# A decoder layer on one core: a wider vector tile and another order of the tile pools

## Chip, cores and metric

The kernel runs on one core of a Trainium2 chip. The metric is device time in microseconds (us) for one execution, from the first instruction to the last and what lies around them. The engines are TensorE (PE in the profile; PEld is its loading of the stationary operand), VectorE (DVE), ScalarE (ACT), GpSimd (POOL) and SyncE (SP, which issues nearly all DMAs). Operands of products lie in the on-chip memory, 128 partitions wide; an address is a byte offset within each partition.

## What is computed

One layer of a decoder trunk, fp32 in and out, for 512 tokens of 1024 features:

```
h = x + 1/2 * SwiGLU_1(RMSNorm(x))                     D_FF 2816
n = RMSNorm(h);  P = n @ W_in + b_in                   1024 -> 6 x 1024
    A: GLU -> causal depthwise conv (31) -> LayerNorm -> swish -> w_a
    B: GELU -> u, v -> LayerNorm(v) -> chunked causal gating u * (W_s v + b) -> w_b
h = h + (sigmoid(gate_A) * y_A + sigmoid(gate_B) * y_B) @ W_out
h = h + CrossAttn(RMSNorm(h), RMSNorm_mem(mem))        4 heads, 256 memory tokens
h = h + 1/2 * SwiGLU_2(RMSNorm(h))
y = RMSNorm_final(h)
```

## The kernel before

Features lie on the partitions and the 512 tokens along them, so a residual or operand tile is 128 x 512. Each matrix product is made of three: activation and weight are each split into a high part (type fp32r) and the rest (fp32r too), and `mm3` adds high by high, high by low and low by high into one PSUM tile (lines 103 to 106). `linear` takes a column tile of weights as the stationary operand and moves the activations (512 columns, 256 for the memory); `linear_rows` (lines 172 to 174) does the reverse, so that there the weights move and the activations are loaded. `linear` works through blocks of 8 K tiles: one DMA of 512 KB into `raw` (4 buffers), then `wsplit`: ScalarE writes `whi` (line 96), VectorE the rest `wlo` (line 97), three buffers each, then 24 products.

The stages in order are: FFN 1 (44 column tiles up, `g` and `u`; 8 down, `d`), the keys of the memory (`pk`), the gated channels (`av`, `ag`), the token-major halves of the input projection (`r`), the spatial gating (`pm`, transposes `pt`) between the products of `gate_b`, `yb`, `ga`, the memory's values, `ya`, `o`, the attention (`pq`, scores `sc`, transposes `ptt`, weighted values `po`, `wo`), FFN 2, and the final norm by halves (`dl`). The convolution (line 344, 30 steps of VectorE for each of 8 channel tiles) stands in pieces behind the blocks of weights from the gated channels on; how many go behind a block is decided by `spend` from the constants MM_US (the three products of a K tile), SPLIT_US (VectorE's part of a block's split) and OP_US (another VectorE operation). The order on each engine is fixed when the program is built.

Where a tile lies follows from the pools, which are laid out one after the other in the order in which they are opened. `const` begins at byte 16512, which is 128 past a multiple of 256. Its first tile is `vec`, all vectors as columns (356 columns of 4 bytes), then `h`, the split activations `xhi` and `xlo`, `ident`, `ones`, `avg` and `mhalf`, four columns of -0.5 that `pow_mhalf` (line 196, on POOL) takes as exponent. `wpool` holds the weights, `tmp` the short-lived tiles, among them some of 4 to 32 bytes, and `big` 50 slots of 128 x 512 for everything else that products read: the split hidden activations `f`, the memory `m`, keys, values, queries, probabilities. Bytes past a multiple of 256, as the programs are built:

| operands | before | after |
|---|---|---|
| `h`, `xhi`, `xlo`, `ident`, `ones`, `avg` | 32 | 0 |
| weights `raw`, `whi`, `wlo` | 64 | 0 |
| slots of `big` | 96 | 0 |
| `acc` and the other tiles `ev` of `tmp` | 64 | 0 |
| `rb` tiles of `tmp` | 224 | 160 |

## Time and profile before

| | |
|---|---|
| median of 3 runs | 1356.39 us (1355.55 to 1356.74) |
| the profiled execution | span 1355.1 us |
| PE busy | 1332.3 us, 98%, 5968 products |
| PEld busy | 1079.1 us, 80% |
| DVE busy | 777.9 us, 57% |
| ACT busy | 456.5 us, 34% |
| DMA | 132.47 MB, mean 98 GB/s |

The profile is of one execution; its span is the time from the first to the last instruction, 1.3 us under the median of the runs. Busy time is the union of an engine's instructions. A matmul's end is modelled and lies beyond the start of the next, so how fast products follow each other is read from their starts, or from how many fall in a stretch, and not from their mean duration. VectorE's instructions overlap in the same way at their ends. An fp32 product of 512 columns is recorded as two instructions.

### The profile page before, as it was taken

What the parts mean: (1) busy time and instruction counts of PE and PEld (TensorE: products, weight loads), DVE (VectorE), ACT (ScalarE), POOL (GpSimd) and SP (SyncE); (2) the same over time, 40 slices, a digit from 0 to 9 for tenths busy, and PEclk for the clock granted to TensorE, in tenths of its full rate; (3) what the DMA queues carried; (4) which work ended last, traced back from release to release, by engine and by line L of the source; (5) the groups of instructions that cost most, each with busy time, mean ns of one, the idle gap of its engine ahead of it and who ended that gap; (6) DMA issues with size and microseconds to landing.
All of it is one profiled execution on the core that took longest, in us unless ns stands there. A gap on an engine that the chain in (4) does not pass through costs nothing.

```text
span 1355.1 us, 14923 instructions
## 1 busy us (share of the span) xinstructions
PE 1332.3 (98%) x5968; PEld 1079.1 (80%) x5968; DVE 777.9 (57%) x1078; ACT 456.5 (34%) x618; POOL 19.4 (1%) x31
## 2 busy tenths in 40 slices
PE   7999999999999999999999999999999999999996
PEld 6788888888898888888787788887878888888886
DVE  5544444434367999998996775554644444442323
ACT  5322222223233223343224743334432222222221
POOL 0000000000020000100000000000000000000000
PEclk9999999999999999999999999999999999999998
DMA  6333333233353332322233333202332333323321
GB/s 207 109 94 93 94 93 94 86 96 109 114 181 115 94 94 94 101 97 76 92 94 116 102 109 109 62 20 76 123 93 93 94 94 93 94 86 101 86 70 62
DMA packets 40660, 132.47 MB, mean 98 GB/s; under 512 B 4432, under 2 KB 7248, under 8 KB 40592
## 3 DMA queue, kind: packets, MB, share of 16 engines
q1 hardware_dynamic: 39872, 129.17, 30.9%
q0 software_dynamic: 720, 2.36, 0.6%
q8 instruction: 46, 0.75, 0.2%
q14 instruction: 22, 0.18, 0.0%
HBM read 129.42 MB, written 2.10 MB: 97 GB/s over the span
## 4 chain that ended last, share of the span: by engine, by line
PE 97%; DVE 1%; ACT 1%; DMA 0%; issue 0%; SPq 0%; DVEq 0%; POOLq 0%; ACTq 0%
PE u L106 6%; PE g L104 6%; PE u L105 6%; PE g L105 6%; PE g L106 6%; PE u L104 6%; PE d L106 6%; PE d L104 6%; PE d L105 6%; PE r L173 2%; PE r L172 2%; PE r L174 2%; PE ya L104 1%; PE ya L105 1%; PE o L105 1%; PE av L105 1%
## 5 line engine op out<-in xcount | busy, mean ns | idle before, releaser
L344 DVE SCALAR_TENSOR_TENSOR cv<-ap,vec,cv 128x494 f32<-128x494 f32 (+24 forms) x240 | 163.3, 729 | 0.4
L244 DVE TENSOR_TENSOR u<-u,n4rb 128x512 f32<-128x512 f32 x22 | 15.2, 692 | 70.3 <-PE u L106 70.3
L244 DVE TENSOR_TENSOR u<-u,n1rb 128x512 f32<-128x512 f32 x20 | 13.8, 691 | 65.8 <-PE u L106 65.8
L240 DVE TENSOR_TENSOR g<-g,n4rb 128x512 f32<-128x512 f32 x22 | 15.2, 692 | 51.7 <-PE g L106 47.5
L240 DVE TENSOR_TENSOR g<-g,n1rb 128x512 f32<-128x512 f32 x20 | 13.8, 691 | 43.3 <-PE g L106 43.3
L246 DVE TENSOR_TENSOR f<-s,u 128x512 f32<-128x512 f32 x44 | 30.4, 692 | 5.4 <-ACT s L242 1.1
L261 DVE SCALAR_TENSOR_TENSOR h<-d,h 128x512 f32<-128x512 f32 x15 | 10.4, 692 | 31.5 <-PE d L106 31.5
L242 ACT ACTIVATE s<-g 128x512 f32<-128x512 f32 x44 | 27.8, 633 | 0.1
L192 DVE TENSOR_TENSOR acc<-acc,sq 128x512 f32<-128x512 f32 x34 | 23.3, 685 | 0.1
L191 ACT ACTIVATE sq<-h 128x512 f32<-128x512 f32 x34 | 21.2, 624 | 1.4 <-DVE h L261 0.2
L184 DVE SCALAR_TENSOR_TENSOR xlo<-h,vec,xhi 128x512 fp32r<-128x512 f32 x24 | 17.7, 746 | 5.3 <-ACT xhi L183 5.2
L183 ACT ACTIVATE xhi<-h,vec 128x512 fp32r<-128x512 f32 x24 | 17.2, 717 | 1.9 <-DVE h L626 1.0
L543 DVE TENSOR_TENSOR h<-o,h 128x512 f32<-128x512 f32 x8 | 5.5, 692 | 13.7 <-PE o L106 13.7
L532 DVE TENSOR_TENSOR ga<-ya,sga 128x512 f32<-128x512 f32 x8 | 5.5, 690 | 13.4 <-PE ya L106 13.4
L387 DVE TENSOR_TENSOR uv<-r,br 128x512 f32<-128x512 f32 x16 | 10.7, 686 | 0.1
L104 PE MATMUL fg<-xhi,first0h 128*128 128x512 f32 x4 | 2.2, 553 | 7.8 <-ACT first0h L96 7.8
L587 ACT ACTIVATE pr<-sc,mx 128x256 f32<-128x256 f32 x16 | 7.4, 470 | 6.4 <-DVE mx L584 6.3
L567 DVE TENSOR_TENSOR qt<-pq,n3rb 128x512 f32<-128x512 f32 x8 | 5.3, 687 | 7.3 <-ACT n3rb L218 4.3
L626 DVE TENSOR_TENSOR h<-wo,h 128x512 f32<-128x512 f32 x8 | 5.4, 688 | 7.0 <-PE wo L106 7.0
L388 ACT ACTIVATE uv<-uv 128x512 f32<-128x512 f32 x16 | 9.0, 621 | 0.6 <-DVE uv L387 0.6
L583 DVE TENSOR_REDUCE mx<-sc 128x2 f32<-128x512 f32 x8 | 5.5, 692 | 3.7 <-PE sc L106 3.3
L97 DVE TENSOR_TENSOR d1w8l<-d1w,d1w8h 128x1024 fp32r<-128x1024 f32 x2 | 2.5, 1226 | 8.7 <-ACT d1w8h L96 8.7
(4300 smaller groups left out, 4279.4 us busy)
## 6 DMA issues: line engine op xcount, KB each, us to landing
h<-xT SPq DMA_DIRECT2D x8, 256.0 KB, 5.9
first<-w_gu SPq DMA_DIRECT2D x8, 256.0 KB, 6.1
d0w<-w_dn SPq DMA_DIRECT2D x4, 512.0 KB, 3.5
d1w<-w_dn SPq DMA_DIRECT2D x4, 512.0 KB, 3.7
d2w<-w_dn SPq DMA_DIRECT2D x4, 512.0 KB, 3.4
d3w<-w_dn SPq DMA_DIRECT2D x4, 512.0 KB, 3.5
d4w<-w_dn SPq DMA_DIRECT2D x4, 512.0 KB, 3.6
d5w<-w_dn SPq DMA_DIRECT2D x4, 512.0 KB, 3.4
```

The lines of the kernel that those rows point to most:

```text
L104: PE.matmul(out, whi, ahi, start=start, stop=False)
L105: PE.matmul(out, whi, alo, start=False, stop=False)
L106: PE.matmul(out, wlo, ahi, start=False, stop=stop)
L172: PE.matmul(accs[t], a_h, whi[:, k - k0, :], start=k == 0, stop=False)
L173: PE.matmul(accs[t], a_h, wlo[:, k - k0, :], start=False, stop=False)
L174: PE.matmul(accs[t], a_l, whi[:, k - k0, :], start=False, stop=k == nk - 1)
L192: V.tensor_tensor(out=acc, in0=acc, in1=sq, op=ALU.add)
L240: V.tensor_tensor(out=g1, in0=pg, in1=rb, op=ALU.mult)
L242: S.activation(s1, g1, AF.Silu)
L244: V.tensor_tensor(out=u1, in0=pu, in1=rb, op=ALU.mult)
L246: V.tensor_tensor(out=f, in0=s1, in1=u1, op=ALU.mult)
L344: V.scalar_tensor_tensor(out=o, in0=aps[i][:, :T - back], scalar=w, in1=o, op0=ALU.mult, op1=ALU.add)
```

## The change

The tile `vec` gets 416 columns (1664 bytes) in place of 356; the load fills the first 356 as before. `mhalf` is no tile of its own any more but four of the new columns of `vec`. The pool `big` is opened before `tmp`, so that the tiles of a few bytes lie behind everything that products read. `const` now puts `h` at byte 18176, and from there on all tiles up to those small ones have lengths that are multiples of 256. No instruction is added, removed or moved on any engine: the built programs have the same rows in the same order with the same waits, but for the name `vec` in place of `mhalf` on POOL. Comments and docstrings are dropped as well, which changes line numbers alone.

```diff
@@ -42,6 +42,7 @@
     VOFF[_n] = _o
     _o += _w
 NV = _o
+VW = 416
...
@@ -52,12 +53,13 @@
     const = ctx.enter_context(tc.tile_pool(name="const", bufs=1))
     wpool = ctx.enter_context(tc.tile_pool(name="wpool", bufs=1))
+    big = ctx.enter_context(tc.tile_pool(name="big", bufs=1))
     tmp = ctx.enter_context(tc.tile_pool(name="tmp", bufs=1))
-    big = ctx.enter_context(tc.tile_pool(name="big", bufs=1))
...
-    vec = const.tile([P, NV], F32, name="vec")
+
+    vec = const.tile([P, VW], F32, name="vec")
...
-    mhalf = const.tile([P, TT], F32, name="mhalf")
+    mhalf = vec[:, NV:NV + TT]
...
-            nc.sync.dma_start(out=vec, in_=vecs)
+            nc.sync.dma_start(out=vec[:, :NV], in_=vecs)
```

## Rows read from the trace of the kernel before

**Rows 1.** The page: span, busy time by engine, granted clock in 40 slices, chain.

```profile
span 1355.1 us, 14923 instructions
...
PE 1332.3 (98%) x5968; PEld 1079.1 (80%) x5968; DVE 777.9 (57%) x1078; ACT 456.5 (34%) x618; POOL 19.4 (1%) x31
...
PEclk9999999999999999999999999999999999999998
...
PE 97%; DVE 1%; ACT 1%; DMA 0%; issue 0%; SPq 0%; DVEq 0%; POOLq 0%; ACTq 0%
```

**Rows 2.** The waits of PE: us in total, times, longest us.

```profile
PE fg L104 <- ACT first0h L96: 7.8, 1, 7.8
PE nf1c L206 <- ACT sq L673: 2.5, 1, 2.5
PE po L104 <- ACT ph L179: 2.3, 4, 0.6
PE nf1b L214 <- DVE nf1d L212: 1.7, 1, 1.7
PE ya L104 <- ACT aa0h L179: 1.3, 1, 1.3
PE yb L104 <- ACT yb5w0h L96: 0.2, 1, 0.2
```

**Rows 3.** Busy time by stretch; in brackets the instructions that touch it.

```profile
core 0: us, PE busy (x) PEld busy (x) DVE busy (x) ACT busy (x) POOL busy (x), PEclk, DMA share, GB/s
60.00:250.00 190.00, 190.00 (x816) 153.00 (x815) 85.23 (x103) 55.87 (x68) 0.00 (x0) 1.00 0.31 94
...
510.00:535.00 25.00, 25.00 (x109) 20.09 (x108) 23.83 (x35) 7.68 (x9) 0.00 (x0) 1.00 0.33 102
...
1195.00:1315.00 120.00, 120.00 (x516) 96.44 (x515) 40.01 (x45) 33.41 (x41) 0.00 (x0) 1.00 0.30 88
```

**Rows 4.** PE in order of time (start, duration), last product: first and last of 28.

```profile
1325.75 0.28 PE L104 MATMUL dl<-f3h,dl0h 128*128 128x256 f32 x1
...
1328.89 0.28 PE L104 MATMUL dl<-f12h,dl8h 128*128 128x256 f32 x1
```

**Rows 5.** PE in order of time, the kernel's start: first and last of 10.

```profile
8.35 0.63 PE L105 MATMUL fg<-xlo,first0h 128*128 128x512 f32 x1
...
12.19 0.63 PE L105 MATMUL fu<-xlo,first0h 128*128 128x512 f32 x1
```

**Rows 6.** PE in order of time: four transposes, one after the other.

```profile
612.66 0.60 PE L444 MATMUL pt<-ident,uv 128*128 128x128 f32 x4
```

**Rows 7.** All transposes of line 444: ns min/median/max, first and last start.

```profile
L444 PE MATMUL pt<-ident,uv x32: 270/272/273, 605.9 to 648.2; 128*128 128x128 f32 x32
```

**Rows 8.** The chain, 649 to 659 us: start, us, what.

```profile
649.09 0.69 DVE ob7l L180
649.78 6.48 DVE cv L344 x10
...
658.03 0.62 DVE yb3w0l L97
```

**Rows 9.** Busy time by stretch, the convolution; columns as in rows 3.

```profile
425.00:557.00 132.00, 132.00 (x567) 106.15 (x566) 126.70 (x183) 37.24 (x44) 2.42 (x3) 1.00 0.31 95
557.00:645.00 88.00, 87.83 (x438) 72.98 (x437) 80.78 (x124) 34.66 (x48) 1.85 (x2) 1.00 0.30 95
645.00:689.00 44.00, 43.58 (x189) 34.27 (x188) 43.76 (x63) 10.10 (x11) 0.00 (x0) 1.00 0.27 87
```

**Rows 10.** The convolution's steps, line 344; columns as in rows 7.

```profile
L344 DVE SCALAR_TENSOR_TENSOR cv<-ap,vec,cv x240: 684/729/750, 422.1 to 707.2; 128x490 f32<-128x490 f32 x7, 128x500 f32<-128x500 f32 x6, 128x494 f32<-128x494 f32 x6, 128x492 f32<-128x492 f32 x6
```

**Rows 11.** Busy time by stretch, the keys; columns as in rows 3.

```profile
387.00:403.00 16.00, 16.00 (x124) 15.10 (x123) 12.33 (x23) 8.89 (x12) 7.09 (x10) 1.00 0.70 197
```

**Rows 12.** PE in order of time, scores of the first head: first and last of four.

```profile
871.83 0.28 PE L104 MATMUL sc<-k0h,q0h 128*128 128x256 f32 x1
...
872.18 0.28 PE L105 MATMUL sc<-k0l,q0h 128*128 128x256 f32 x1
```

## Prediction

> **What bounds the kernel now.** I read the page first: TensorE has work in 98% of the span, and the chain that ended last runs over it for 97% [rows 1]. Busy time alone would not prove a bound, since matmul ends are modelled; the table of waits does. TensorE waits 7.8 us for the first weights, 2.3 us for four operands of the attention, 1.3 us for the first operand of w_a, 4.2 us in the last norm, and next to nothing elsewhere [rows 2]. So for some 1,330 us the time is the number of products times their spacing, and the next view is the spacing, which is a count over a stretch. In 60 to 250 us (FFN up, moving xhi and xlo) 816 products touch 190 us; the first of them started up to 0.4 us earlier, so the spacing is 190.4/816 = 0.2333 us. In 510 to 535 us (linear_rows, moving weights) it is 25.4/109 = 0.233 us, in 1195 to 1315 us (FFN down, moving f tiles) 120.4/516 = 0.2333 us [rows 3]. The granted clock is 1.00 in all three, the 2.4 GHz level, at which 512 columns are 213.3 ns. Every product of 512 columns thus takes **20 ns too long**, 9.4%, in all three roles. That is the only thing in this kernel that is large.

> What kind of loss is it? Three rows narrow it down. Products of 256 columns are spaced (1328.89 - 1325.75)/27 = 0.1163 us against 106.7 ns: 9.6 ns too long, half as much for half the columns [rows 4]. So it is a rate, some 2.5 ns for each 64 columns, which are 256 bytes of a partition, and not a fixed price of an instruction or of its weight load, which is 128 columns in both. The first products of the kernel, 8.35 to 12.19 us, are spaced 3.84/9 = 0.427 us, which is 512 columns at the 1.2 GHz level, with **no loss** [rows 5]. And the four fp32 transposes that follow each other span 0.60 us, the last being 0.27 us long, so their spacing is 0.33/3 = 0.109 us: 128 columns at two cycles each are 106.7 ns, a remainder of 2.3 ns [rows 6, 7]. At half the byte rate, by either road, the loss is gone. It sits where the operand is fetched at 4 bytes a cycle of 2.4 GHz.

> **The change part by part.** No instruction moves: the rows of PE, DVE, ACT and SP are the same in both programs, waits included, and on POOL only the name mhalf becomes vec. The memset of the -0.5 columns and the load of the other 356 columns of vec write separate columns, the load keeps its 1424 bytes a partition, and no instruction waits for more than before. These edits cost nothing, and need no cover. What moves is addresses: the moving operands lie 32, 64 or 96 bytes past a multiple of 256 before, and none lies on one; all of them do after. VectorE's tmp tiles go the other way in part (the rb tiles at 160 past a multiple); VectorE and ScalarE are priced as they are.

> The trace has no product with an operand on a multiple of 256, so the price of one is bounded from both sides. From above by 233.3 ns (the start does not matter), from below by 213.3 ns (the columns alone). I take **215.6 ns**, columns plus the 2.3 ns of the transposes, the only stream at this clock that shows no loss by columns. My reason: the loss goes in steps of 256 bytes, as if a fetch of that size that starts off a boundary touched two lines; it must then go when every fetch starts on one. That 32, 64 and 96 bytes off lose the same fits, since each of them straddles every time. A weak witness beside it: the planner's constants in the code fit the trace for VectorE (OP_US 0.66; ten convolution steps in 6.48 us [rows 8]) but not for TensorE (MM_US 0.65 for three products, where three now take 0.70). 0.65/3 is 216.7 ns.

> [...]

> The sum. The code issues 5358 products of 512 columns in fp32r (per FFN 1056 up; 528 down in the first, 462 in the second; 384 gated channels; 384 token-major; 192 each for gate_b, w_b, gate_a, w_a, w_out, w_q, w_o; 96 values; 48 weighted) and 468 of 256 (192 keys, 48 spatial gating, 96 scores, 132 in the last product). Twelve are at the lower clock. 5346 x (233.3 - 215.6 = 17.7 ns) = 94.6 us; 468 x (116.3 - 109.0 = 7.3 ns) = 3.4 us; together **98.0 us**, if TensorE stays the bound everywhere.

> Where does it not? VectorE in the middle, where the convolution fills the room behind the products. Busy there: 126.7 of 132 us, 80.8 of 88, 43.8 of 44 [rows 9]. With 566 products of 512 in the first stretch TensorE would want 132 - 10.0 = 122.0 us, 4.7 less than VectorE is busy; in the third 44 - 3.3 = 40.7 us, 3.1 less; in the second nothing. If busy were occupancy, 7.8 us would be lost. But it is not: a convolution step lasts 729 ns and ten in a row take 6.48 us, 648 ns each [rows 8, 10]; at 648/729 the 126.7 us are 113, under TensorE's 122. Only at 648 to 659 us is the path VectorE itself, ten steps ahead of the split of yb3 [rows 8]; the 44 us around it save little, and I charge 2 us. The four heads wait for ph already (2.3 us), and two fills of 24 products shrink by 0.42 us each per head, at most 3.4 us; half, 1.7. At 387 to 403 us the key products draw 197 GB/s with the DMA engines 70% busy [rows 11]; they would draw 7% more, I charge 0.6 us; with no gain there at all it would be 192 x 7.3 ns = 1.4 us. Together 4.3 us lost, 1 at the least, 12.6 at the most (7.8 + 3.4 + 1.4).

> 98.0 - 4.3 = 93.7 us. The profiled span of 1355.1 us becomes 1261.4 us; the median of the runs is 1.3 us over that span, so **1262.7 us**. This case's own range: the spacing from 213.3 ns to 217.9 ns (twice the remainder) moves it by 12.3 us either way, and the losses by -3.3 to +8.3: 1247 to 1283 us.

> **The rivals.** *Nothing changes.* The fetch of 4 bytes per column simply runs at 8.8 bytes per ns (2048/233.3), whatever the start: a limit of the port explains half-clock, fp32 and the proportion as well as mine does. For it: 32, 64 and 96 bytes off are the same, no row gets better with a better start. Against it: the transposes and the cold products only show that the limit lies above 4.8 bytes per ns, so nothing decides. 1356.4 us. [...]

> *Half of it.* Port and straddling share the loss: 224.5 ns, gain 5346 x 8.8 ns + 1.7 us - 1.5 us = 47 us, 1309 us; with the split between a quarter and three quarters, 1286 to 1332 us.

> *Slower.* With all tiles on the same boundary the moving stream and the weight load (512 bytes a partition, two steps of 256) start at the same place in a line and collide. Price: two steps of 2.5 ns on 5826 products, 29 us, 1385 us; it decides only if the alignment itself gives less than 5 ns. Against it: in the scores both operands lie 96 bytes past a multiple today, and are spaced (872.18 - 871.83)/3 = 0.117 us, as others of 256 columns are [rows 12].

> **How the numbers follow.** Full gain 0.75 (the 256-byte step and its absence at half rate are what straddling predicts; the port's limit would have to be 512/560 of the clock by chance), half 0.09, nothing 0.12, slower 0.04. The time is the first one's, 1262.7 us. Its own range holds 0.71 of the 0.75; with the half case, up to 1332 us, 0.80. So 1247 to 1332 us. Faster by over 0.2%, which is about what a measurement of this kernel can tell from no change: 0.84; same 0.12; slower 0.04.

> **What would show it.** Right: 0.2156 us in all three stretches of rows 3, 0.109 us in the last product, 0.427 us unchanged at the start, and TensorE's waits longer by a few us, at yb3, at the four ph and nowhere else. VectorE's mean durations should stay (729 ns). Wrong: a spacing of 0.2333 us again (port), or a value between in all of them (half); a TensorE that waits for VectorE through 425 to 557 us would mean that busy was occupancy, and the time near 1270 us. A granted clock under 1.00 at the higher rate would take the gain back in another way; before, it stays at 1.00 through every dense stretch.

## Result and profile after

The changed kernel takes 1323.91 us (median of three executions; 1323.03 to 1324.05), beside 1355.97 us (1355.13 to 1356.74) for the kernel before: a ratio of 0.9763, 95% interval 0.9747 to 0.9779. A fourth execution took 6179.85 us, for which nothing on record gives a cause, and is left out. The gain is 32.1 us, a third of the 93.7 that were forecast. The time lies within the range, in the case called half of it, and not where the likeliest case put it. The profiled execution has a span of 1322.3 us, 32.8 less than [rows 1].

The page of the changed kernel, its parts as in [rows 1], and the waits of PE as in [rows 2] (all line numbers from the pools on are two higher):

```profile
span 1322.3 us, 14923 instructions
...
PE 1299.4 (98%) x5968; PEld 1079.5 (82%) x5968; DVE 776.7 (59%) x1078; ACT 456.3 (35%) x618; POOL 19.4 (1%) x31
...
PEclk9999999999999999999999999999999999999998
...
PE 97%; DVE 1%; ACT 1%; DMA 0%; issue 0%; SPq 0%; DVEq 0%; POOLq 0%; ACTq 0%
```

```profile
PE fg L106 <- ACT first0h L98: 8.2, 1, 8.2
PE nf1c L208 <- ACT sq L675: 2.5, 1, 2.5
PE po L106 <- ACT ph L181: 2.3, 4, 0.6
PE nf1b L216 <- DVE nf1d L214: 1.7, 1, 1.7
PE ya L106 <- ACT aa0h L181: 1.3, 1, 1.3
```

TensorE is the bound as before and waits no longer than before but for 0.4 us at the first weights. VectorE, ScalarE and the weight loads are busy for as long as before. So nothing ate the missing 62 us: the products are just not as fast as forecast. Busy time by stretch says so, for the three roles of [rows 3] (FFN up, linear_rows, and FFN down in 1210 to 1290 us):

```profile
60.00:240.00 180.00, 180.00 (x795) 149.05 (x795) 82.53 (x98) 54.16 (x66) 0.00 (x0) 1.00 0.31 97
...
500.00:525.00 25.00, 25.00 (x112) 20.72 (x111) 24.44 (x35) 10.51 (x14) 0.00 (x0) 1.00 0.27 89
...
1210.00:1290.00 80.00, 80.00 (x355) 66.26 (x354) 24.26 (x27) 22.59 (x26) 0.00 (x0) 1.00 0.29 84
```

With the same 0.4 us for the product that had begun, the spacing is 180.4/795 = 0.2269 us, 25.4/112 = 0.2268 and 80.4/355 = 0.2265, where [rows 3] gave 0.2333. It is one value in all three roles at a granted clock of 1.00, and it is neither the 0.2156 of the forecast nor the 0.2333 of no change.

The last product, 256 columns, went the other way. PE in order of time, first and last of 35 starts:

```profile
1292.80 0.28 PE L106 MATMUL dl<-f1h,dl0h 128*128 128x256 f32 x1
...
1296.88 0.28 PE L107 MATMUL dl<-f12l,dl8h 128*128 128x256 f32 x1
```

4.08/34 = 0.1200 us, against 0.1163 in [rows 4] and 0.109 forecast. An explanation by which every product gains from a better start cannot hold: these have it, and lost 3.7 ns each.

### The profile page after: what moved, and what is told of

Same layout as the page of the kernel before. It is cut to its first block, busy times and chain, and to the rows that moved or that the text cites. A ratio compares the mean times of both kernels' runs of the same rounds, so it can differ in the third digit from the quotient of the medians.

```text
span 1322.3 us, 14923 instructions
## 1 busy us (share of the span) xinstructions
PE 1299.4 (98%) x5968; PEld 1079.5 (82%) x5968; DVE 776.7 (59%) x1078; ACT 456.3 (35%) x618; POOL 19.4 (1%) x31
## 4 chain that ended last, share of the span: by engine, by line
PE 97%; DVE 1%; ACT 1%; DMA 0%; issue 0%; SPq 0%; DVEq 0%; POOLq 0%; ACTq 0%
PE g L106 6%; PE u L107 6%; PE g L107 6%; PE u L106 6%; PE u L108 6%; PE g L108 6%; PE d L106 6%; PE d L108 6%; PE d L107 6%; PE r L175 2%; PE r L176 2%; PE r L174 2%; PE ya L106 1%; PE ya L107 1%; PE gb L108 1%; PE ga L106 1%
## 5 line engine op out<-in xcount | busy, mean ns | idle before, releaser
L545 DVE TENSOR_TENSOR h<-o,h 128x512 f32<-128x512 f32 x8 | 5.5, 692 | 12.5 <-PE o L108 12.5
L534 DVE TENSOR_TENSOR ga<-ya,sga 128x512 f32<-128x512 f32 x8 | 5.5, 689 | 12.3 <-PE ya L108 12.3
```

## Experiments

"Distance" below is the start of the loaded operand less the start of the moving one, modulo 256 bytes. In the changed kernel it is 0 everywhere; in the kernel before it is +32 (up) or -32 (linear_rows, down), and 0 where one slot of `big` meets another. Five of the kernels below leave the layer out and run groups of products alone, on one tile `mov` that moves and one tile `sta` that is loaded, both fp32r. Their code is shown abridged, and the edits of the layer are shown against the changed kernel. The spacings in text and tables are means over the starts of a group without its first four intervals, because a group that follows another takes some products to settle: `mbsb` below starts with intervals of 236, 224, 231 and 235 ns and ends at 226.7. In a row of a whole group, settling included, the spacing is the length less the last product's own (0.39 us at 512 columns, 0.28 at 256 and fewer) over 23, or over 47 in groups of 48, and can differ by up to some 1.5 ns.

### A map of starts

```diff
+OFFS = (0, 32, 64, 96, 128, 160, 192, 224)
+for i, mo in enumerate(OFFS):
+    for j, so in enumerate(OFFS):          # name: m, a to h for mo, s, a to h for so
+        for r in range(24):
+            m0, s0 = mo // 4 + r % 4 * 512, so // 4 + r % 8 * 128
+            PE.matmul(acc, sta[:, s0:s0 + 128], mov[:, m0:m0 + 512], ...)
```

> A stream of products alone, nothing else of the layer: 64 groups of 24 fp32r products of 512 columns, group mXsY with the moving operand X and the loaded operand Y bytes past a multiple of 256 (a to h are 0, 32, 64, 96, 128, 160, 192, 224). In the layer the spacing is 233.3 ns with all operands off the multiples and 226.7 ns with all on them. Theory 'moving': the moving operand's start alone decides, so the eight groups with X = a are spaced 226.7 ns whatever Y is, and the other 56 are spaced 233.3. Theory 'loaded': only the eight with Y = a are at 226.7. Theory 'both': only masa is at 226.7 and the other 63 are at 233.3. Theory 'distance': what counts is how far the two lie apart, so the eight groups with X = Y are at 226.7 too, and some other distance may lie below, at 215.6 ns.

Measured, over the 64 groups:

| distance, bytes | spacing, ns (lowest to highest of 8 pairs) |
|---|---|
| 0 | 226.6 to 227.3 |
| 32 | 233.1 to 233.4 |
| 64 | 233.3 to 233.5 |
| 96 | 234.2 to 234.3 |
| 128 | 232.6 to 233.6 |
| 160 | 233.2 to 233.6 |
| 192 | 228.7 to 229.0 |
| 224 | 233.3 to 233.4 |

Some of the groups in order of time (start, length):

```profile
24.42 5.61 PE L30 MATMUL masa<-mov,sta 128*128 128x512 f32 x24
29.87 5.75 PE L30 MATMUL masb<-mov,sta 128*128 128x512 f32 x24
...
57.88 5.67 PE L30 MATMUL masg<-mov,sta 128*128 128x512 f32 x24
...
74.58 5.64 PE L30 MATMUL mbsb<-mov,sta 128*128 128x512 f32 x24
...
224.95 5.61 PE L30 MATMUL mese<-mov,sta 128*128 128x512 f32 x24
```

`masb` has its moving operand on a multiple of 256 and is slow; `mbsb` has both operands 32 past one and is fast. Where an operand lies does not matter, only the distance of the two: once settled, the eight pairs of a distance agree within 1 ns. No pair comes near 215.6 ns.

### What the rest hangs on: sizes, type, neighbours

The second kernel runs the same groups with both starts on a multiple (`on`) and 32 and 64 past one (`off`), and varies one thing at a time.

```diff
+for n in (64, 128, 192, 256, 320, 384, 448, 512): group(0, 0, "on", n=n); group(32, 64, "off", n=n)
+for c in (32, 64, 96, 128): group(0, 0, "onc", c=c); group(32, 64, "offc", c=c)      # loaded columns
+group(..., mk=1, sk=1)                    # the same operands each time
+group(..., m=movb, s=stab, size=2)        # bf16
+# 20 adds of VectorE, then 12 copies of ScalarE, beside a group
```

> Products alone again, groups on (both operands at multiples of 256) and off (moving at 32, loaded at 64), a to h with 64 to 512 columns in steps of 64. In the layer 256 and 512 columns on the multiples are spaced 120.0 and 226.7 ns, 13.3 ns over the columns at 2.4 GHz in both; off them 116.5 and 233.3 ns, 9.8 and 20 over. Theory 'fixed rest': on the multiples each product pays 13.3 ns whatever its columns (173.3 at 384, 66.7 at 128), off them 9.4% (175.0 at 384, 58.3 at 128), so off is the faster one below some 340 columns. Theory 'weight load': the rest is paid for the bytes of the loaded operand, so with 64 loaded columns in place of 128 (oncb) it halves and the spacing is 220.0; theory 'instruction': it stays 226.7 there. With the same operands again and again (onsame) no change by either. bf16 (bfon, bfoff): 215.6 ns by both, as its moving operand is half the bytes; if 226.7, the rest has nothing to do with bytes. VectorE or ScalarE at work beside the products (vec, act against lone): 226.7 in all three unless the rest is a collision with their accesses, in which case lone is lower.

```profile
69.23 5.52 PE L38 MATMUL offc<-mov,sta 128*128 128x192 f32 x48
...
100.11 8.49 PE L38 MATMUL onf<-mov,sta 128*128 128x384 f32 x48
108.44 8.49 PE L38 MATMUL offf<-mov,sta 128*128 128x384 f32 x48
...
136.30 11.08 PE L38 MATMUL onh<-mov,sta 128*128 128x512 f32 x48
147.22 11.36 PE L38 MATMUL offh<-mov,sta 128*128 128x512 f32 x48
...
169.69 5.68 PE L38 MATMUL oncb<-mov,sta 128*64 128x512 f32 x24
...
213.89 10.53 PE L38 MATMUL bfon<-movb,stab 128*128 128x512 bf16 x47
...
234.62 5.40 PE L38 MATMUL bfonn<-movb,stab 128*128 128x256 bf16 x48
239.86 5.40 PE L38 MATMUL bfoffn<-movb,stab 128*128 128x256 bf16 x48
...
250.59 11.04 PE L38 MATMUL vec<-mov,sta 128*128 128x512 f32 x48
261.47 11.04 PE L38 MATMUL act<-mov,sta 128*128 128x512 f32 x48
```

| columns | on, ns | off, ns | columns at 2.4 per ns, ns |
|---|---|---|---|
| 256 | 119.9 | 118.3 | 106.7 |
| 320 | 146.7 | 146.6 | 133.3 |
| 384 | 173.4 | 173.3 | 160.0 |
| 448 | 202.7 | 204.5 | 186.7 |
| 512 | 227.1 | 233.2 | 213.3 |

The rate of 2.4 columns per ns behind the last column, and behind the 2.4 GHz of the prediction, is measured here: in bf16 the columns from 256 to 512 add 215.8 - 109.2 = 106.6 ns, and fp32r at distance 0 adds 227.1 - 119.9 = 107.2. At distance 0 the spacing is the columns plus about 13.3 ns at 256, 320, 384 and 512 columns (16.0 at 448): a fixed rest, and not the 9.4% for which the forecast took it. The off column shows how that mistake came about: at 512 columns some 6 ns come on top, at 384 none for this pair of starts, and at 256 the whole loss is a little less than the rest, so that between 512 and 256 alone the loss looks like a rate. Fewer loaded columns (64: 229.8 ns), the same operands each time (226.7), VectorE at work beside (226.65) or ScalarE (226.65) leave the rest in place. In bf16 it is gone, and these two pairs of starts do not differ: 215.8 ns for 512 columns (of `bfon` one start is missing from the trace, so its 10.53 us hold 47 intervals) and 109.2 for 256, on and off alike. So the 215.6 ns of the forecast hold for bf16 within 0.2 ns, and not for fp32r. Of the groups of 64 to 192 columns most ran at a granted clock of 0.50 (0.64 in the mean over 40 to 78 us). `offc` did not: 192 columns at 1.00 are spaced 111.7 ns, where the columns are 80.0, and the weight loads are busy for all of 69.3 to 74.5 us. With 64 columns `ona` has the same 111.7 ns while it is at 1.00, and at 0.50 both 64 and 128 columns have 213.3. So at 192 columns and fewer it is not the moving columns that set the spacing, and the fixed rest is a statement on 256 and more.

### The layer with every operand 32 bytes past a multiple

If the distance is all that counts, the gain must stay when no operand lies on a multiple of 256.

```diff
-VW = 416
+VW = 360
```

> The changed kernel with vec 360 columns wide in place of 416: every operand of every product then lies 32 bytes past a multiple of 256, moving and loaded alike, and none on one. Theory 'multiples of 256' (the change as described, and the prediction's straddling fetch): no fetch starts on a boundary, so all is as in the kernel before, spacing 233.3 ns, 1356 us. Theory 'distance' (only the distance between the starts of the moving and the loaded operand counts, modulo 256): the distance is 0 everywhere, spacing 226.7 ns, 1324 us as the changed kernel.

1324.71 us (1322.84 to 1324.83), ratio to the kernel before 0.9769, interval 0.9753 to 0.9785: the time of the changed kernel, and its rows (60 to 240 us and FFN down, columns as above):

```profile
60.00:240.00 180.00, 180.00 (x796) 149.04 (x795) 82.53 (x98) 54.18 (x66) 0.00 (x0) 1.00 0.32 97
1210.00:1290.00 80.00, 80.00 (x355) 66.24 (x354) 24.27 (x27) 22.59 (x26) 0.00 (x0) 1.00 0.29 84
```

This settles it for the layer: lying on multiples of 256 gives nothing by itself. It is one way to bring all operands to the same residue.

### The two halves of the change

With `vec` widened alone, `xhi`, `xlo` and the weights have residue 0, and the slots of `big` 32, so that FFN up and linear_rows have distance 0, and FFN down has -32 as before.

```diff
-    big = ctx.enter_context(tc.tile_pool(name="big", bufs=1))
     tmp = ctx.enter_context(tc.tile_pool(name="tmp", bufs=1))
+    big = ctx.enter_context(tc.tile_pool(name="big", bufs=1))
```

> The changed kernel with the pools in the old order: activations xhi and xlo and the weights lie on multiples of 256, the slots of big 32 past. By 'distance' the 3456 products of 512 columns that read xhi or xlo (g, u, av, ag, r, gb, ga, pq) are spaced 226.7 ns, those between slots and weights (d, yb, ya, o, wo, pv) stay at 233.3: 3456 x 6.67 ns = 23.0 us less than before, 1333 us. By 'multiples of 256, both operands' the same; by 'moving operand alone' the r products too and the same within 3 us; so this run sizes the part, it does not part the theories.

1334.24 us (1334.00 and 1334.48), ratio 0.9843, interval 0.9824 to 0.9863. With the pools exchanged alone, weights and slots share the residue 64 and `xhi` stays at 32:

```diff
-    vec = const.tile([P, VW], F32, name="vec")
+    vec = const.tile([P, NV], F32, name="vec")
...
-    mhalf = vec[:, NV:NV + TT]
+    mhalf = const.tile([P, TT], F32, name="mhalf")
...
-            nc.sync.dma_start(out=vec[:, :NV], in_=vecs)
+            nc.sync.dma_start(out=vec, in_=vecs)
```

> The changed kernel with vec and mhalf as before: xhi and xlo 32 past a multiple of 256, weights and slots 64 past. By 'distance' the products between slots and weights (d, yb, ya, o, wo, pv: 1854 of 512 columns) have distance 0 and are spaced 226.7 ns, those with xhi and xlo have 32 and stay at 233.3; the keys and the last product, 324 of 256 columns, go from 116.6 to 120.0 ns: 1854 x 6.67 - 324 x 3.4 ns = 11.3 us less than before, 1345 us. By 'multiples of 256' nothing lies on one: 1356 us.

1346.33 us (1346.10 and 1346.56), ratio 0.9932, interval 0.9913 to 0.9952. Busy time by stretch, of the first and then of the second:

```profile
60.00:240.00 180.00, 180.00 (x796) 149.05 (x795) 82.53 (x98) 54.14 (x66) 0.00 (x0) 1.00 0.31 97
1210.00:1290.00 80.00, 80.00 (x345) 64.26 (x344) 24.62 (x27) 23.47 (x28) 0.00 (x0) 1.00 0.33 95
```

```profile
60.00:240.00 180.00, 180.00 (x774) 145.00 (x773) 81.10 (x97) 52.49 (x64) 0.00 (x0) 1.00 0.31 94
1210.00:1290.00 80.00, 80.00 (x354) 66.27 (x353) 25.33 (x28) 22.72 (x28) 0.00 (x0) 1.00 0.33 97
```

In both stretches a half speeds up just the products whose distance it makes 0: up 796 against 774, down 345 against 354. In the second kernel no operand lies on a multiple of 256 either. Beside the kernel before in the same comparison (1355.21 us) the halves gain 21.0 and 8.9 us, together 29.9, where the version 32 bytes on gains 30.5. The expected 23.0 and 11.3 us lie within the intervals, which are some 2.6 us wide either way.

### Why the distance counts: three guesses that fell

The next three kernels ask for a mechanism. The first loads every first, second, third or fourth column, so that the 128 loaded columns span up to four times the bytes; it also tries distances of a few bytes.

```diff
+for so in (4, 8, 16, 24): group(so, 1, "fine")
+for step in (1, 2, 3, 4):
+    loaded = sta[:, s0:s0 + 128 * step].rearrange("p (c s) -> p c s", s=step)[:, :, 0]
```

> Products alone, moving operand on a multiple of 256; the loaded operand at a to h = 0 to 224 past one, its 128 columns 1, 2, 3 or 4 elements of 4 bytes apart (groups one, two, three, four); fine a to d is step 1 at 4, 8, 16, 24 bytes; narrow is step 2 with 256 moving columns. Theory 'overtaking': the moving stream takes 8 bytes per cycle of 1.2 GHz and the load 4, so while the next operand is loaded the one passes the other two or three times in the same 256 bytes, and each pass costs 8 cycles (2 passes: 226.7 ns, 3: 233.3). With step 2 both go at 8 bytes per cycle and never pass: most of two are spaced 215.6 ns (narrow 109), and perhaps one or two offsets, where they would start in the same place, stay dear. With steps 3 and 4 the load is the faster one and passes again: 220 to 233. Theory 'fixed rest': the load costs what it costs by its 128 columns, and two, three and four read as one does, 226.7 or 233.3 by offset; if the bytes that it spans count, two to four are dearer. fine: 226.7 up to some offset if the place is coarser than 32 bytes, 233.3 from the first step if it is exact.

```profile
24.54 5.74 PE L33 MATMUL finea<-mov,sta 128*128 128x512 f32 x24
...
46.79 5.63 PE L33 MATMUL onea<-mov,sta 128*128 128x512 f32 x24
...
108.06 5.68 PE L33 MATMUL twod<-mov,sta 128*128 128x512 f32 x24
```

The map comes again at step 1 (226.8 at 0, 228.9 at -64, otherwise 233.2 to 234.3). Four bytes apart costs nearly as much (232.4) as 32, and 8, 16 and 24 bytes cost 230.7 to 233.3, so the distance has to be 0 exactly. With a step of 2 no distance comes down to 226.7 (230.0 to 233.7, the lowest at 64 and 96), with 3 and 4 they are worse (233.2 to 240.0). At 256 columns and a step of 2 all distances have 119.8 to 121.1. The guess asked for 215.6 at a step of 2, and it fell. Its two rates agree with the runs: 4 bytes per column at 2.4 columns per ns are 9.6 bytes per ns, and a load of 128 columns takes 79 ns longer than one of 32 (`m5_pairs_and_loads` below), 384 bytes at 4.9 bytes per ns. That one stream passes the other, and what a pass costs, is the author's guess and not shown.

The second reads the moving operand, and writes the output, from the last column to the first. The guess behind it was that the two streams delay each other where they pass, so that turning one of them round would bring some groups down to 215.8 ns.

```diff
-PE.matmul(out, loaded, moving, ...)
+PE.matmul(out[:, ::-1], loaded, moving[:, ::-1], ...)
```

> Products alone as in m3_steps, but the 512 moving columns are read from the last to the first, and written to PSUM from the last to the first, so that the result is the same. The loaded operand is 1 to 4 elements apart from column to column (reone, retwo, rethree, refour), at a to h = 0 to 224 bytes past a multiple of 256; nreone and nretwo move 256 columns. [...] Theory 'fixed rest': the load takes its share of reads in any order, and the best is 226.7 again, at another offset.

```profile
25.21 5.76 PE L34 MATMUL reonea<-mov,sta 128*128 128x512 f32 x24
...
70.02 5.76 PE L34 MATMUL retwoa<-mov,sta 128*128 128x512 f32 x24
```

All 32 groups of 512 columns give 233.2 to 233.5 ns, whatever the distance and the step. Backwards costs what an unequal start costs, and at 512 columns the place of the loaded operand no longer matters; at 256 it does (117.6 to 120.5). Whether the reading or the writing does it is not shown, since both were turned.

The third lets two starts alternate, so that a product's moving operand fits its own loaded operand (`own`) or that of the next one, whose load runs beside it (`next`; in the kernel before the load for the product of 13.40 us starts at 13.17, beside the product of 13.16), 64 or 128 bytes apart; and it loads 96, 64 and 32 columns, and moves 384, at all eight distances.

```diff
+group([(0, 0), (64, 64)], "ownnear");   group([(0, 64), (64, 0)], "nextnear")
+group([(0, 0), (128, 128)], "ownfar");  group([(0, 128), (128, 0)], "nextfar")
+for c in (96, 64, 32):
+    for so in OFFS: group([(0, so)], ..., c=c)
+for so in OFFS: group([(0, so)], ..., n=384)
```

> Products alone, read forwards. Four groups alternate between two pairs of starts (moving, loaded), in bytes past a multiple of 256: ownnear (0,0),(64,64); ownfar (0,0),(128,128); nextnear (0,64),(64,0); nextfar (0,128),(128,0). Theory 'next load': what counts is the moving stream of a product against the load of the product after it, which goes on beside it; then nextnear and nextfar, whose next load starts where the stream does, are spaced 226.7 ns, ownfar 233.5, and ownnear (233.5 + 228.8)/2 = 231.2, by the rows of the map for +64 and -64. Theory 'own load': a product's own pair counts, and it is the other way round: ownnear and ownfar 226.7, nextfar 233.5, nextnear 231.2. Then most, half and quarter load 96, 64 and 32 columns instead of 128, at a to h = 0 to 224 bytes past a multiple, moving at 0: by 'weight load' the best of half is spaced 220.0 ns (half of the 13.3 over the columns) and the best of quarter 216.6, at some offset, which the first sizes at one offset alone could have missed; by 'fixed rest' the best is 226.7 in each. mid moves 384 columns at a to h: 173.3 at all offsets if the loss comes in whole steps that 384 columns don't show, else 173.3 at a and about 177 elsewhere.

```profile
36.24 5.64 PE L31 MATMUL ownfar<-mov,sta 128*128 128x512 f32 x24
41.72 5.68 PE L31 MATMUL nextfar<-mov,sta 128*128 128x512 f32 x24
...
113.79 5.62 PE L31 MATMUL halfd<-mov,sta 128*64 128x512 f32 x24
...
146.87 5.87 PE L31 MATMUL quarterb<-mov,sta 128*32 128x512 f32 x24
...
206.88 4.40 PE L31 MATMUL midf<-mov,sta 128*128 128x384 f32 x24
```

Of the same kernel, the weight loads grouped by name (busy us, mean ns of one | idle before):

```profile
L31 PEld LDWEIGHTS same<-mov,sta 128*128 128x128 f32 x24 | 4.5, 188 | 1.0
...
L31 PEld LDWEIGHTS quartera<-mov,sta 128*32 128x32 f32 x24 | 2.6, 109 | 2.9
```

Neither pairing is fast: `own` gives 231.7 and 228.5, `next` 231.5 and 230.0, so it is not one neighbour that has to fit. The best distance moves with the number of loaded columns: 0 for 128, 64 for 96 columns (228.2), 96 for 64 columns (226.7), and 96 or 128 for 32 columns (230.5, 230.8). So the loaded stream takes part in the 6.6 ns. But a shorter load does not take the rest of 13.3 ns away: a load of 32 columns takes 109 ns in place of 188, and nothing falls below 226.7. With 384 moving columns the distance counts for less: 173.3 to 174.8 ns at 0, 32, 64, 96 and 192 bytes, 176.1 to 176.8 at 128, 160 and 224.

## Why the prediction was wrong

**What bounds the kernel: right.** Products times spacing was the whole time before and is after. The waits of TensorE are unchanged to 0.4 us, and the granted clock stayed at 1.00 in the stretches of 226.5 to 226.9 ns.

**The loss as a rate: wrong.** The prediction compared 512 columns with 256 and read 2.5 ns for each 64 columns. The sizes in between, which no row of before has, show two terms: a fixed 13.3 ns, and at 512 columns 6.6 ns from unequal starts. Two points fit a rate and a sum as well; the reason that was built on the rate, a fetch of 256 bytes that straddles a boundary, was not in the rows at all, and it fails in both directions: a moving operand on a multiple is slow beside a loaded one that is 32 past (`masb`), and the layer with no operand on a multiple is as fast as the changed kernel.

**The spacing on multiples, 215.6 ns: wrong, and with it the sum.** This is the term that failed. It measured 226.7, so that 6.6 of the 17.7 ns came. The sum with the right terms: 5298 x 6.6 ns = 35.0 us, less 324 products of 256 columns (192 keys, 132 last) x 3.7 ns = 1.2, is 33.8; the spans differ by 32.8. The 48 products of the weighted values, the scores and the spatial gating pair one slot of `big` with another, had distance 0 before and do not count. The 2.3 ns of the transposes [rows 6, 7] did not carry over to fp32r products. The rows show 0.109 us for a transpose of 128 columns; that this is two cycles a column and a remainder is the author's reading. The 2.3 ns need not be a price of the moving columns at all: each transpose loads 128 columns for 128 that move, and fp32r products of few columns are spaced 111.7 ns in `ona` and `offc`, whether 64 or 192 move. No run parts the two readings.

**32, 64 and 96 off lose the same: the right rows, read for one theory.** The three roles of [rows 3] have equally slow products because each pairs unequal starts, and so they fit the distance as well as straddling. Two groups of products told the two apart. One was used for something else: in the scores both operands lie 96 past a multiple. Four starts to two decimals [rows 12] gave 0.117, "as others". The scores of the second head, in order of time, are 24 in a row (first and last, kernel before):

```profile
889.38 0.28 PE L104 MATMUL sc<-k1h,q2h 128*128 128x256 f32 x1
...
892.13 0.28 PE L106 MATMUL sc<-k1h,q3l 128*128 128x256 f32 x1
```

2.75/23 = 0.1196 us, not the 0.1163 of [rows 4]: the spacing that the last product has after the change was there before, at equal starts and off any multiple. Three intervals at a resolution of 0.01 us leave 3 ns open, and the difference in question was 3 ns. The other group, the weighted values of 512 columns, was not read. Of the ten in a row in the first head, once they have settled (kernel before):

```profile
887.80 0.39 PE L105 MATMUL po<-pl,vm01h 128*128 128x512 f32 x1
...
889.16 0.39 PE L106 MATMUL po<-ph,vm01l 128*128 128x512 f32 x1
```

1.36/6 = 0.2267 us: the spacing that 512 columns have after the change was in the trace before it, at equal starts 96 past a multiple. It is the price that the prediction looked for and called missing from the trace.

**The rivals.** The half case has the time (1309 us, 1286 to 1332), but not its mechanism, a port limit and straddling sharing the loss. That the time went the way that was forecast is luck: the edit that put every start on a multiple of 256 also made the starts of each pair equal, and only the second counts. Nothing changes was wrong for this kernel, and right for the alignment as such: the version at 32 bytes (1324.71 us, beside 1323.91) shows that multiples give nothing. The slower rival had the place (both streams starting alike) and the wrong sign for 512 columns; for 256 it had even the sign, 3.7 ns. Its dismissal by [rows 12] rested on the same reading. A limit of the port, a straddling fetch and two streams that collide were guesses, and no run shows any of them. Shown is that the two operands are not independent in time: for fp32r the start of the one relative to the other is worth 6.6 ns of 233.3.

**The losses: hardly tested.** VectorE did not become the bound of the convolution's longest stretch. Busy time by stretch, where [rows 9] had 126.7 of 132 us:

```profile
413.00:540.00 127.00, 127.00 (x562) 105.21 (x561) 124.52 (x179) 38.44 (x45) 2.41 (x3) 1.00 0.31 98
```

TensorE is busy all 127 us, with VectorE at 98%. The order on PE is the same in both kernels, so the products can be followed: those that start from 425.03 to 557.10 us before start from 414.77 to 543.07 after, 128.3 us in place of 132.1, which is the whole 566 x 6.6 ns. Whether busy is occupancy was not put to the test by that, as the 126.7 us of VectorE fit under 128.3 either way. The 188 from 645.08 us on, 180 of them of 512 columns, take 43.2 us in place of 44.0, 0.8 of 1.2 us. The convolution's steps kept their length (731 ns, before 729), and the ten steps ahead of the split of yb3 are still on the chain, which ran there as in [rows 8]:

```profile
634.36 6.46 DVE cv L346 x10
...
642.61 0.45 DVE yb3w0l L99
```

The four waits for ph stayed at 2.3 us in all. At a third of the gain the products of a head still cover what they covered, so the 4.3 us of losses were neither shown nor refuted; 33.8 less 32.8 leaves 1.0.

**Right besides:** the first products, some 0.43 us apart, did not change. PE in order of time at the kernel's start, first and last of nine:

```profile
8.78 0.63 PE L107 MATMUL fg<-xlo,first0h 128*128 128x512 f32 x1
...
12.20 0.63 PE L108 MATMUL fg<-xhi,first0l 128*128 128x512 f32 x1
```

3.42/8 = 0.427 us, as in [rows 5]: 1.2 columns per ns, with weight loads of 0.33 us in place of 0.19. The granted clock reads 1.00 there (8 to 12.5 us of the kernel before, 8 to 13 us of the changed one), so the lower clock of the prediction is its author's reading of the spacing; in `m2_sizes` loads of 333 ns go with a granted clock of 0.50. Four transposes follow each other in 0.60 us, as in [rows 6].

**What stays open.** The cause of the fixed rest, and how equal starts save 6.6 ns. Shown is that the rest is the same at 256, 320, 384 and 512 columns (but 16.0 ns at 448), that at 512 columns fewer loaded columns, other steps, repeated operands and other engines at work do not bring it lower, and that bf16 does not have it. In bf16 the moving columns have half the bytes and the loads are shorter (98 ns, against 188) at once, and no run parts these. No pair of starts was found with less than 226.7 ns for 512 columns of fp32r. Bringing the keys and the last product back to unequal starts would give 324 x 3.7 ns = 1.2 us, an estimate from the spacings above and less than can be measured here; it was not tried.

## What to carry to other kernels

Compare the spacing of products with the time of their columns (2.4 per ns here), at more than two sizes, before calling a loss a rate. In a kernel of fp32r products of 512 columns and 128 loaded ones, let the tile that moves and the tile that is loaded start at the same place modulo 256 bytes (226.7 ns, against 232.6 to 234.3 at six of the other seven distances); which of the eight places of the map is all the same (226.6 to 227.3; at 256 columns equal starts cost 3.7 ns instead), and a pool of tiles of odd lengths ahead of one of them undoes it (with `tmp` ahead of `big`, 1334.24 us in place of 1323.91). When a change of layout is to be priced, list the residues of both operands of every group of products, look for a group that already has the new relation, and read its spacing over as many starts as it has; a map of all offsets takes one short kernel.
